# Contracting two key groups of an input projection in halves, the first halves beside the modulation that produces their operand

## The chip, the cores and the metric

One core of a Trainium2 chip runs the whole program once. The metric is the device time of one execution in microseconds (us). The engines are TensorE (PE in the profile, PEld for its weight loads), VectorE (DVE), ScalarE (ACT), GpSimd (POOL) and SyncE (SP), which here only issues DMA transfers. Each engine takes its instructions in the order in which they stand in its queue.

## The reference

A diffusion backbone of two layers works on 256 latent and 256 context tokens of width 2048. The first layer begins so:

```python
sh1, sc1, g1, sh2, sc2, g2 = jnp.split(silu(c) @ ada_w[l] + ada_b[l], 6, axis=-1)
h  = rmsnorm(x_lat, norm_mix[l]) * (1 + sc1) + sh1        # 256 x 2048
hc = the same for x_ctx, with c_ctx                       # 256 x 2048
# even mixer: one input projection, then segments ka, va, kb, vb, a, b, qa, qb, za
pc = hc @ w_in[:, :n_ctx];  p = h @ w_in
ka, va, qa = silu(depthwise_conv(5 taps))                 # gated DeltaNet: k, v, q
k = rope(l2norm(heads(ka)))                               # 8 heads of 128
```

Then come the chunked gated delta rule in both directions (first the context tokens, whose final state starts the latent ones), neighbourhood attention, an output projection, a gated feed-forward part, and the second layer with a short convolution in place of the mixer.

## The kernel before

A product in float32 is made of three TensorE products: weights and activations are split into a high part (`whi`, `h_hi`) and the rest (`wlo`, `h_lo`), and high x high, high x low and low x high are summed in PSUM. ScalarE makes `whi` (L173), VectorE subtracts for the first 576 columns of `wlo` (L241) and GpSimd for the other 448 (L243). Weight tiles of 128 x 1024 (two of the 16 contraction steps of a 512-column group) come through a ring of four `raw` buffers, and two `whi` and two `wlo`.

`fm_stream` (L297 on) contracts one group of 512 columns: a step of it takes one block of 128 rows of `h`, and issues 24 matmuls of 128 x 256 (L311), or 20 with four 512-wide ones (L307) in the first step. It holds four PSUM banks (`mm`, four in all) until `evac` has taken them. The last two steps are issued together, bank by bank.

The program opens with the first modulation, in eight blocks. `start_block(b)` loads 4 MB of `ada_w` (tile `araw0`, four buffers) and multiplies it by the two condition vectors (L484, tile `gd`); `start_tokens(b)` copies the result (L490, `mrow`), turns it to columns (L495), transposes two blocks of normalised tokens (L192, `xn`) and makes blocks 2b and 2b+1 of `h` (L508 to L510, tiles `hlhi`, `hchi`, `hllo`, `hclo`, and `h0` for block 0). So block k of `h` exists only after modulation block k // 2. After each of the first seven blocks, two steps of the first key group (KA0, `s0`, columns C_KA on) are issued on the blocks of `h` just made. After the eighth, `drive(s0)` issues the last two steps, and the second key group (KA1) follows in 16 steps, with one step of a later modulation (`pump`; its DVE part is L338) to each.

`head_evac` (L568) takes a key group further: it copies the four PSUM banks to SBUF (`hst`, alternately on ScalarE and VectorE), and defers nine pieces of work that `drive` spreads over the next steps: for each of the four heads the convolution (`cv`, L560 to L565), then transposes, squares and their sums (L591, L592), and last the norm and the rotation (L606 to L617) and a store to DRAM (`kd`). Behind KA1 stand the gates: a small product (L690 to L698) and a chain of small VectorE operations (L710 to L750), and then what is still deferred. `chunk_matrices(1)` and `inverses` (L862 to L898) use KA0 and KA1 from `kd`; the streams of the query and value groups (QA, VA) are written after them in the program.

The program text gives each instruction a place, and the framework's scheduler, which has a timing model of its own, moves instructions past each other to fill what it takes for gaps. So the order in each queue is that of the built program, not of the text.

Of the kernel before, what the change touches and what calls it, by code (L numbers as in the profile page):

```python
# [29 lines left out]
D = 2048  # L30
KT = D // 128
FH = 5632
# [77 lines left out]
def body(tc, x, c, ctx, c_ctx, ada_w, ada_b, norm_mix, norm_ffn, ffn_w_gate, ffn_w_up, ffn_w_down,  # L110
# [186 lines left out]
    def fm_stream(segs, ks, ws, evac, cut=None):  # L297

        ps = [None] * 4
        for i, group in grouped(((k, (k, hi, lo)) for k, hi, lo in w_steps(segs, ks, cut)), len(ks)):  # L300
            for f in range(4):
                if i == 0:
                    ps[f] = mmt()
                for g, (k, hi, lo) in enumerate(group):
                    a, b = hi[:, f * 128:(f + 1) * 128], lo[:, f * 128:(f + 1) * 128]
                    if i == 0:
                        PE.matmul(ps[f][:, 0:len(ws) * 256], a, h0[:, 0:len(ws) * 256], start=True, stop=False)  # L307
                    for j, (wt, mv) in enumerate(((a, h_hi), (a, h_lo), (b, h_hi))):
                        for n, w in enumerate(ws):
                            if j or i:  # L310
                                PE.matmul(ps[f][:, n * 256:(n + 1) * 256], wt, mv(w, k), start=False,  # L311
                                          stop=i == len(ks) - 1 and g == len(group) - 1 and j == 2 and w == ws[-1])
                if i == len(ks) - 1:
                    evac(f, ps[f])
# [109 lines left out]
    h0 = hlp.tile([128, 512], F32R, name="h0")  # L424
    hs_hi = (hlp.tile([128, KT - 1, 256], F32R, name="hlhi"), hcp.tile([128, KT - 1, 256], F32R, name="hchi"))
    hs_lo = (hlp.tile([128, KT, 256], F32R, name="hllo"), hcp.tile([128, KT, 256], F32R, name="hclo"))

    def h_hi(w, k):
        return hs_hi[w][:, k - 1, :] if k else h0[:, w * 256:(w + 1) * 256]
# [8 lines left out]

    st = Stack()
# [48 lines left out]
    def start_tokens(b, pr):  # L488
        mrow = sp.tile([128, 512], F32, name="mrow", tag="mrow", bufs=2)
# [12 lines left out]
        for k in range(2 * b, 2 * b + 2):  # L502
# [3 lines left out]
            for w in range(2):  # L506
                m = sp.tile([128, 256], F32, name="modt", tag="modt", bufs=4)
# [4 lines left out]
    def token_stats():  # L512
# [5 lines left out]
        junk = sp.tile([128, D], F32, name="junk")  # L518
# [49 lines left out]
    def head_evac(n, q, c0, done, sums):  # L568
# [3 lines left out]
        def f(i_, p):  # L572
            st_[i_] = kvp.tile([128, 512], F32, name="hst", tag="hst", bufs=4)[:, 0:n * 128]
            copy(st_[i_], p[:, 0:n * 128])
# [52 lines left out]
    def ka_evac(q):  # L627
# [3 lines left out]
        return head_evac(4, q, 0, done, True)  # L631
# [20 lines left out]

    sums = start_block(0)
    token_stats()
    s0 = fm_stream([(wv, C_KA, 512)], ks, [0, 1], ka_evac(0))
    for b in range(8):
        start_tokens(b, sums)
        if b < 7:
            next(s0), next(s0)
            sums = start_block(b + 1)  # L660
    st.close()
    rstk = Stack()
# [13 lines left out]
    drive(fm_stream([(wv, C_KA + 512, 512)], ks, [0, 1], ka_evac(1)), pump, R_KA)  # L676
# [175 lines left out]
    def inverses(parts, q):  # L852
# [7 lines left out]
        xdT = gw.tile([128, 16, 128], F32, name="xdT", tag="xdT", bufs=XDT)  # L860
# [539 lines left out]
```

## Time and profile before

| | |
|---|---|
| three runs | 2948.97, 2952.24 and 2953.81 us; median 2952.24 us |
| profiled execution | 2949.88 us, of it a span of 2947.9 us from its first to its last instruction |
| busy share of the span | PE 94%, PEld 78%, DVE 65%, ACT 45%, POOL 20% |
| read from DRAM | 657.63 MB, 230 GB/s over the span |

The span is that of the instructions of the program; the time of the execution is 2.0 us longer. A matmul counts as busy from its issue to its modelled end, and the next is issued before that, so the busy share of PE is not its use: what it lost is read from the idle time before its instructions, and from the granted clock. The changed part of the program lies in the first 150 us; what follows from it reaches to about 480 us.

### The profile page before, as it was taken

How to read it: one execution, taken by the hardware profiler on the slowest of the kernel's cores; microseconds unless marked ns; L12 is line 12 of the kernel's file. 1: busy time of each engine (PE TensorE's matmuls, PEld its weight loads, DVE VectorE, ACT ScalarE, POOL GpSimd, SP SyncE). 2: the span in 40 equal slices, each digit the busy share in tenths (PEclk: the TensorE clock that was granted, in tenths of full speed). 3: DMA queues.
4: the chain of work that ended last, by engine and by line, in shares of the span. 5: the costliest groups of instructions: out<-in, count | busy, mean ns of one | idle time of the engine just before them, and what ended most of it. 6: DMA issues, size and time to landing. Idle time of an engine off the chain costs nothing. (4 is left out here: it accounts for less than half of the span.)

```text
span 2947.9 us, 40712 instructions
## 1 busy us (share of the span) xinstructions
PE 2764.4 (94%) x15113; PEld 2295.6 (78%) x15113; DVE 1901.8 (65%) x2409; ACT 1337.0 (45%) x1822; POOL 596.2 (20%) x431
## 2 busy tenths in 40 slices
PE   6998888989899899999999998899999999999997
PEld 3697888978777778888878777777778888888886
DVE  2378786744457777666777767777767546445675
ACT  3245444333355444544445555344454444444554
POOL 1157535335241111100111101111111001000010
PEclk9998999999999999999999999999999999999999
DMA  9955657765657688877778766878658657656553
GB/s 343 289 162 160 185 177 251 232 205 184 180 155 262 236 298 294 293 266 270 268 273 274 252 204 234 285 268 297 211 177 315 199 184 257 188 182 220 192 192 123
DMA packets 284930, 680.82 MB, mean 231 GB/s; under 512 B 57273, under 2 KB 97313, under 8 KB 283323
## 3 DMA queue, kind: packets, MB, share of 16 engines
q1 hardware_dynamic: 262148, 652.48, 66.6%
q10 hardware_dynamic: 22583, 25.73, 2.9%
q8 instruction: 119, 1.95, 0.3%
q14 instruction: 80, 0.66, 0.1%
HBM read 657.63 MB, written 20.48 MB: 230 GB/s over the span
## 5 line engine op out<-in xcount | busy, mean ns | idle before, releaser
L241 DVE TENSOR_TENSOR wlo<-raw,whi 128x1024 fp32r<-128x1024 f32 (+1 forms) x800 | 998.0, 1260 | 530.7 <-ACT whi L173 499.2
L173 ACT ACTIVATE whi<-raw 128x1024 fp32r<-128x1024 f32 x800 | 835.8, 1056 | 668.0 <-PE mm L285 479.4
L338 DVE SCALAR_TENSOR_TENSOR acc<-araw,cT,acc 128x1024 f32<-128x1024 f32 (+1 forms) x312 | 366.5, 1175 | 248.7 <-DMA araw<-in_ada_w_dram 222.3
L283 PE MATMUL mm<-wlo,fhi 128*128 128x512 f32 x1232 | 477.7, 393 | 2.1 <-DVE wlo L241 2.0
L282 PE MATMUL mm<-whi,fhi 128*128 128x512 f32 x1232 | 475.9, 397 | 0.0
L285 PE MATMUL mm<-whi,flo 128*128 128x512 f32 x1232 | 392.4, 392 | 0.0
L336 POOL TENSOR_TENSOR acc<-araw,acc 128x1024 f32<-128x1024 f32 (+1 forms) x78 | 159.0, 2039 | 1068.6 <-ACT araw L335 599.5
L283 PEld LDWEIGHTS mm<-wlo,fhi 128*128 128x128 f32 x1232 | 232.4, 189 | 53.7 <-DVE wlo L241 5.0
L285 PEld LDWEIGHTS mm<-whi,flo 128*128 128x128 f32 x1232 | 231.6, 188 | 50.6
L282 PEld LDWEIGHTS mm<-whi,fhi 128*128 128x128 f32 x1232 | 232.7, 189 | 48.4
L282 PE MATMUL mm<-whi,ahi 128*128 128x512 f32 x672 | 262.3, 395 | 4.0 <-DVE rtmp L1157 2.9
L283 PE MATMUL mm<-wlo,ahi 128*128 128x512 f32 x672 | 261.9, 393 | 0.2 <-DVE wlo L241 0.2
L243 POOL TENSOR_TENSOR wlo<-raw,whi 128x448 fp32r<-128x448 f32 x112 | 163.4, 1460 | 285.7 <-ACT whi L173 267.3
L285 PE MATMUL mm<-whi,alo 128*128 128x512 f32 x672 | 211.7, 395 | 2.8 <-DVE alo L177 2.6
L335 ACT ACTIVATE araw<-araw,cT 128x1024 f32<-128x1024 f32 (+1 forms) x78 | 74.4, 954 | 256.3 <-DMA araw<-in_ada_w_dram 235.2
L311 PE MATMUL mm<-hllo,whi 128*128 128x256 f32 x640 | 184.1, 293 | 0.0
L311 PE MATMUL mm<-hlhi,wlo 128*128 128x256 f32 x600 | 168.3, 296 | 14.1 <-DVE wlo L241 10.6
L311 PE MATMUL mm<-hlhi,whi 128*128 128x256 f32 x600 | 170.4, 296 | 5.8 <-ACT whi L173 4.2
L1159 POOL TENSOR_TENSOR xs<-rtmp,xs 128x512 f32<-128x512 f32 x24 | 35.4, 1493 | 633.2 <-DVE rtmp L1157 631.9
L282 PEld LDWEIGHTS mm<-whi,ahi 128*128 128x128 f32 x672 | 127.0, 189 | 32.9 <-issue 3.4
L285 PEld LDWEIGHTS mm<-whi,alo 128*128 128x128 f32 x672 | 126.2, 189 | 32.7 <-DVE alo L177 5.7
L283 PEld LDWEIGHTS mm<-wlo,ahi 128*128 128x128 f32 x672 | 126.8, 189 | 29.5 <-DVE wlo L241 2.0
(398 smaller groups left out, 4694.0 us busy)
## 6 DMA issues: line engine op xcount, KB each, us to landing
araw<-in_ada_w_dram SPq DMA_DIRECT2D x288, 512.0 KB
raw<-in_ffn_w_down_dram SPq DMA_DIRECT2D x176, 512.0 KB
raw<-in_ffn_w_gate_dram SPq DMA_DIRECT2D x160, 512.0 KB
raw<-in_ffn_w_up_dram SPq DMA_DIRECT2D x160, 512.0 KB
raw<-in_ev_w_in_dram SPq DMA_DIRECT2D x112, 512.0 KB
araw<-in_ada_w_dram SPq DMA_DIRECT2D x192, 256.0 KB
raw<-in_od_w_in_dram SPq DMA_DIRECT2D x96, 512.0 KB
raw<-in_ev_w_out_dram SPq DMA_DIRECT2D x32, 512.0 KB
```

What stands on the lines that cost most here:

```text
L173: ACT.activation(dst, src, AF.Copy)
L241: DVE.tensor_tensor(lo[:, 0:cut], raw[:, 0:cut], hi[:, 0:cut], op=OP.subtract)
L243: POOL.tensor_tensor(lo[:, cut:], raw[:, cut:], hi[:, cut:], op=OP.subtract)
L282: PE.matmul(ps[ti][n], a, hi[:, n * 512:(n + 1) * 512], start=first, stop=False)
L283: PE.matmul(ps[ti][n], a, lo[:, n * 512:(n + 1) * 512], start=False, stop=False)
L285: PE.matmul(ps[ti][n], b, hi[:, n * 512:(n + 1) * 512], start=False, stop=last)
L311: PE.matmul(ps[f][:, n * 256:(n + 1) * 256], wt, mv(w, k), start=False, stop=i == len(ks) - 1 and g == len(group) - 1 and j == 2 and w == ...
L335: ACT.activation(raw, raw, AF.Copy, scale=col)
L336: POOL.tensor_tensor(acc2, raw, acc2, op=OP.add)
L338: DVE.scalar_tensor_tensor(acc, raw, col, acc, op0=OP.mult, op1=OP.add)
L1159: eng.tensor_tensor(v, tmp, v, op=OP.add)
```

## The change

`fm_stream` is called four times in place of two. `half(c0)` contracts the first eight blocks of `h` for KA0 and then for KA1 and copies the four sums of each to SBUF (`part`, 128 x 4 x 512). `ka_evac` of the second halves adds `part` to the PSUM bank (one VectorE operation a bank, line 584 of the changed kernel) where it copied the bank before. The modulation blocks 0 to 2 issue two steps each as before, and the blocks 3 to 6 four in place of two: 22 in place of 14. Block 8 of `h` gets a 512-wide tile of its own (`h8`), since it opens a stream now. `mrow` has one buffer in place of two, `modt` three in place of four, and the scratch of the token statistics lies in `hllo`. `part` takes the two buffers of `xdT`, which `inverses` uses later.

```diff
-                        PE.matmul(ps[f][:, 0:len(ws) * 256], a, h0[:, 0:len(ws) * 256], start=True, stop=False)
+                        PE.matmul(ps[f][:, 0:len(ws) * 256], a, lead[k][:, 0:len(ws) * 256], start=True, stop=False)
...
-    h0 = hlp.tile([128, 512], F32R, name="h0")
+    lead = {k: hlp.tile([128, 512], F32R, name=f"h{k}") for k in (0, KH)}
...
+    rstk = Stack()
+    xp = pool("sums", stack=rstk, side="right")
...
-        mrow = sp.tile([128, 512], F32, name="mrow", tag="mrow", bufs=2)
+        mrow = sp.tile([128, 512], F32, name="mrow", tag="mrow", bufs=1)
...
-                m = sp.tile([128, 256], F32, name="modt", tag="modt", bufs=4)
+                m = sp.tile([128, 256], F32, name="modt", tag="modt", bufs=3)
...
-        junk = sp.tile([128, D], F32, name="junk")
+        junk = hs_lo[0][:, 0:KH, :].rearrange("p k t -> p (k t)")
...
-            copy(st_[i_], p[:, 0:n * 128])
+            if part is None:
+                copy(st_[i_], p[:, 0:n * 128])
+            else:
+                DVE.tensor_tensor(st_[i_], p, part[:, i_, :], op=OP.add)
...
+    def half(c0):
+
+        part = xp.tile([128, 4, 512], F32, name="part", tag="xdT", bufs=XDT)
+        return part, fm_stream([(wv, c0, 512)], ks[:KH], [0, 1], lambda f, p: copy(part[:, f, :], p))
...
-    s0 = fm_stream([(wv, C_KA, 512)], ks, [0, 1], ka_evac(0))
+    p0, a0 = half(C_KA)
+    p1, a1 = half(C_KA + 512)
+    s0 = fm_stream([(wv, C_KA, 512)], ks[KH:], [0, 1], ka_evac(0, p0))
+    plan = [s for s, n in ((a0, KH), (a1, KH), (s0, KH)) for _ in range(n)]
     for b in range(8):
         start_tokens(b, sums)
         if b < 7:
-            next(s0), next(s0)
+            for _ in range((2, 2, 2, 4, 4, 4, 4)[b]):
+                next(plan.pop(0))
             sums = start_block(b + 1)
...
-    drive(fm_stream([(wv, C_KA + 512, 512)], ks, [0, 1], ka_evac(1)), pump, R_KA)
+    drive(fm_stream([(wv, C_KA + 512, 512)], ks[KH:], [0, 1], ka_evac(1, p1)), pump, R_KA)
...
-        xdT = gw.tile([128, 16, 128], F32, name="xdT", tag="xdT", bufs=XDT)
+        xdT = xp.tile([128, 16, 128], F32, name="xdT", tag="xdT", bufs=XDT)
```

So in the changed program the queues stand otherwise from the fifth modulation block on. TensorE, in the kernel before, around the columns of that block (`mrow`): the matmuls of the modulation (`gd`) stand right before those that turn its result.

```order
L311 MATMUL mm<-hlhi,wlo 128x256
L311 MATMUL mm<-hchi,wlo 128x256
L484 MATMUL gd<-araw_663,cT_120 32x512 x4
L484 MATMUL gd<-araw_670,cT_120 32x512 x4
L484 MATMUL gd<-araw_677,cT_120 32x512 x4
L495 MATMUL sm<-cs,mrow 128x2 x4
L192 MATMUL sm<-cs,xn 128x128 x4
L484 MATMUL gd<-araw_776,cT_120 32x512 x4
```

TensorE of the changed kernel at the same place (the lines have other numbers: 501 is L495 of before, 193 is L192, 312 is L311):

```order
L312 MATMUL mm<-hllo,whi 128x256
L312 MATMUL mm<-hclo,whi 128x256
L312 MATMUL mm<-hlhi,wlo 128x256
L312 MATMUL mm<-hchi,wlo 128x256
L312 MATMUL mm<-hlhi,whi 128x256
L312 MATMUL mm<-hchi,whi 128x256
L501 MATMUL sm<-cs,mrow 128x2 x4
L193 MATMUL sm<-cs,xn 128x128 x4
L312 MATMUL mm<-hllo,whi 128x256
L312 MATMUL mm<-hclo,whi 128x256
```

Here 26 matmuls of a key group stand between the last `gd` and `mrow`, and 18 between the two halves of the transposes; it is so in the fifth, sixth and seventh block. In the eighth `mrow` follows `gd` directly, as before.

VectorE of the changed kernel, where KA1's sums are taken from PSUM (line 584 is the new addition, 569 is L563 of before, a tap of the convolution, 339 is L338, the pump, 242 is L241, a weight split, 602 is L592):

```order
L242 TENSOR_TENSOR wlo<-raw,whi 128x576
L584 TENSOR_TENSOR hst<-mm,part 128x512
L339 SCALAR_TENSOR_TENSOR acc<-araw,cT,acc 128x512
L584 TENSOR_TENSOR hst<-mm,part 128x512
L569 SCALAR_TENSOR_TENSOR cv<-hst,evcT,cv 128x2x255
L602 TENSOR_REDUCE hss<-sq 128x4
L339 SCALAR_TENSOR_TENSOR acc<-araw,cT,acc 128x512
L569 SCALAR_TENSOR_TENSOR cv<-hst,evcT,cv 128x2x254
L242 TENSOR_TENSOR wlo<-raw,whi 128x576
L339 SCALAR_TENSOR_TENSOR acc<-araw,cT,acc 128x512
L569 SCALAR_TENSOR_TENSOR cv<-hst,evcT,cv 128x2x254
L584 TENSOR_TENSOR hst<-mm,part 128x512
```

The convolution of KA0 is still under way there; in the kernel before it was complete when KA1's copies stood in this queue.

TensorE of the kernel before in the first inverse of the context tokens (L883, L890 and L896 are its products), with matmuls of the value stream between them:

```order
L890 MATMUL gd<-xdT,Y 32x32 x32
L896 MATMUL gd<-Y,xdT 32x32 x32
L192 MATMUL sm<-cs,cv 128x128 x4
L883 MATMUL gd<-xd,n_2286 64x64
L311 MATMUL mm<-hlhi,whi 128x256
L311 MATMUL mm<-hllo,whi 128x256
L311 MATMUL mm<-hlhi,whi 128x256
L311 MATMUL mm<-hllo,whi 128x256
```

TensorE of the changed kernel there (902, 909 and 915 are L883, L890 and L896 of before):

```order
L902 MATMUL gd<-xd,n_2274 32x32
L193 MATMUL sm<-cs,cv 128x128 x4
L902 MATMUL gd<-xd,n_2274 32x32 x31
L909 MATMUL gd<-xdT,Y 32x32 x32
L915 MATMUL gd<-Y,xdT 32x32 x32
L902 MATMUL gd<-xd,n_2273 64x64 x16
L909 MATMUL gd<-xdT,Y 64x64 x16
L308 MATMUL mm<-h_100,whi 128x256
```

In the kernel before 64 matmuls of streams stand within the first inverse and 34 within the second; in the changed one none and 81.

## Rows read from the trace of the kernel before

**Rows 1.** The page, part 1: busy us (share), instructions

```profile
PE 2764.4 (94%) x15113; PEld 2295.6 (78%) x15113; DVE 1901.8 (65%) x2409; ACT 1337.0 (45%) x1822; POOL 596.2 (20%) x431
```

**Rows 2.** Stretches: us, busy us (instructions) by engine, PEclk, DMA share, GB/s

```profile
89.00:144.00 55.00, 48.94 (x362) 33.44 (x361) 18.35 (x52) 12.17 (x20) 10.77 (x7) 0.94 0.90 284
...
144.00:222.00 78.00, 74.10 (x600) 72.68 (x600) 60.19 (x88) 34.57 (x47) 41.46 (x32) 0.98 0.52 163
222.00:300.00 78.00, 65.34 (x471) 62.65 (x470) 67.74 (x110) 43.52 (x69) 57.31 (x52) 0.89 0.49 156
300.00:480.00 180.00, 154.95 (x1642) 149.28 (x1642) 137.09 (x233) 80.27 (x124) 83.99 (x79) 0.95 0.64 196
```

**Rows 3.** PE in order of time: start, us, instruction, [idle before <-releaser]

```profile
71.59 0.28 PE L311 MATMUL mm<-hclo,whi 128*128 128x256 f32 x1
71.71 0.28 PE L311 MATMUL mm<-hlhi,wlo 128*128 128x256 f32 x1
...
92.44 1.07 PE L484 MATMUL gd<-araw,cT 128*32 128x512 f32 x8 [1.27 <-DMA araw<-in_ada_w_dram]
94.42 1.84 PE L495 MATMUL sm<-cs,mrow 128*128 128x2 f32 x8 [0.91 <-DVE mrow L490]
...
140.06 0.74 PE L311 MATMUL mm<-hlhi,whi 128*128 128x256 f32 x4 [1.17 <-DVE hlhi L509]
```

**Rows 4.** One stretch more, columns as in rows 2

```profile
94.20:101.00 6.80, 6.58 (x30) 4.62 (x31) 1.99 (x9) 1.80 (x4) 0.00 (x0) 0.50 1.08 355
```

**Rows 5.** Waits of PE from 89 to 144 us: total us, times, longest

```profile
PE sm L495 <- DVE mrow L490: 3.6, 4, 0.9
```

**Rows 6.** Stretches, DVE alone: us, busy us, PEclk, DMA share, GB/s

```profile
144.00:180.00 36.00, 34.46 (x39) 1.00 0.62 193
180.00:222.00 42.00, 25.72 (x50) 0.96 0.44 137
222.00:297.00 75.00, 66.52 (x104) 0.89 0.48 152
```

**Rows 7.** DVE in order of time: KA0's copy, gates, KA1's rotation

```profile
144.98 0.69 DVE L170 COPY hst<-mm 128x512 f32<-128x512 f32 x1 [2.78 <-PE mm L311]
...
210.27 0.29 DVE L710 COPY ab<-sm 128x128 f32<-128x128 f32 x1 [3.51 <-PE sm L698]
...
223.04 0.29 DVE L740 SCALAR_TENSOR_TENSOR g_t<-gu,ea 128x32 f32<-128x32 f32 x2
...
295.62 1.37 DVE L617 TENSOR_TENSOR hq<-hq,rope 128x256 f32<-128x256 f32 x1
```

**Rows 8.** Groups of DVE, 144 to 297 us: count | busy us, mean ns | idle

```profile
L241 DVE TENSOR_TENSOR wlo<-raw,whi 128x576 fp32r<-128x576 f32 x26 | 28.2, 1084 | 12.6 <-ACT whi L173 12.5
L338 DVE SCALAR_TENSOR_TENSOR acc<-araw,cT,acc 128x512 f32<-128x512 f32 x24 | 24.5, 1022 | 0.5 <-DMA araw<-in_ada_w_dram 0.5
...
L170 DVE COPY hst<-mm 128x512 f32<-128x512 f32 x4 | 2.7, 683 | 2.8 <-PE mm L311 2.8
...
L592 DVE TENSOR_REDUCE hss<-sq 128x2 f32<-128x256 f32 x4 | 1.6, 406 | 0.0
```

**Rows 9.** Lines 241 and 338 (140 to 300 us) and 1157: ns min/median/max

```profile
L241 DVE TENSOR_TENSOR wlo<-raw,whi x26: 745/810/1703, 151.4 to 294.9; 128x576 fp32r<-128x576 f32 x26
...
L338 DVE SCALAR_TENSOR_TENSOR acc<-araw,cT,acc x24: 653/764/1645, 146.7 to 289.6; 128x512 f32<-128x512 f32 x24
...
L1157 DVE TENSOR_TENSOR rtmp<-mm,row x32: 673/681/692, 939.9 to 2932.8; 128x512 f32<-128x512 f32 x32
```

**Rows 10.** POOL in order of time: the clearing of xdT

```profile
136.31 3.54 POOL L862 MEMSET xdT<- 128x2048 f32 x2
```

**Rows 11.** PE in the two inverses, 429 to 459 us, as rows 3

```profile
429.11 0.72 PE L890 MATMUL gd<-xdT,Y 32*32 32x32 f32 x62 [1.64 <-ACT Y L173]
...
435.07 0.30 PE L883 MATMUL gd<-xd,n 64*64 64x64 f32 x2 [3.69 <-DVE xd L898]
...
458.58 0.37 PE L896 MATMUL gd<-Y,xdT 32*32 32x32 f32 x19 [3.26 <-issue]
```

More of the change, by code (lines that the diff above doesn't have):

```diff
@@ L31 @@
 KT = D // 128
+KH = KT // 2
 FH = 5632
@@ L422, in body @@
     hcp = pool("h_ctx", stack=hcstk)
-    h0 = hlp.tile([128, 512], F32R, name="h0")
-    hs_hi = (hlp.tile([128, KT - 1, 256], F32R, name="hlhi"), hcp.tile([128, KT - 1, 256], F32R, name="hchi"))
+    lead = {k: hlp.tile([128, 512], F32R, name=f"h{k}") for k in (0, KH)}
+    hs_hi = (hlp.tile([128, KT - 2, 256], F32R, name="hlhi"), hcp.tile([128, KT - 2, 256], F32R, name="hchi"))
     hs_lo = (hlp.tile([128, KT, 256], F32R, name="hllo"), hcp.tile([128, KT, 256], F32R, name="hclo"))
     def h_hi(w, k):
-        return hs_hi[w][:, k - 1, :] if k else h0[:, w * 256:(w + 1) * 256]
+        if k in lead:
+            return lead[k][:, w * 256:(w + 1) * 256]
+        return hs_hi[w][:, k - 1 - (k > KH), :]
     def h_lo(w, k):
@@ L566, in conv_silu, with head_evac @@
         return o
-    def head_evac(n, q, c0, done, sums):
+    def head_evac(n, q, c0, done, sums, part=None):
         st_ = {}
@@ L625, in to_features, with ka_evac @@
             copy(dst[:, g * 2:g * 2 + 2, :], pt.rearrange("p (i e) -> p i e", i=2))
-    def ka_evac(q):
+    def ka_evac(q, part=None):
         def done(kt, ss):
@@ L630, in done @@
             ACT.dma_start(hslice(kd, 0, 4, q), kt.rearrange("p t h e -> p t (h e)"))
-        return head_evac(4, q, 0, done, True)
+        return head_evac(4, q, 0, done, True, part)
     def va_evac(q):
@@ L658, in body @@
         if b < 7:
-            next(s0), next(s0)
+            for _ in range((2, 2, 2, 4, 4, 4, 4)[b]):
+                next(plan.pop(0))
             sums = start_block(b + 1)
     st.close()
-    rstk = Stack()
     adap = pool("ada", stack=rstk, side="right")
```

## The prediction

> **What bounds the kernel now.** I read the page first: TensorE is busy 94% of the span [rows 1], so over the whole program the question is where TensorE still loses time. I then cut the stretch that the change can reach into four windows [rows 2]. From 89 to 144 us the second half of the modulation runs; DMA is at 0.90 of its engines there and moves 284 GB/s, and it moves 355 GB/s where it is full [rows 4]. So TensorE and DMA are both near their limits, and neither leaves much room. From 222 to 300 us TensorE is held by others: VectorE is busy 67.7 of 78 us and the granted clock is 0.89 [rows 2].
>
> TensorE's own rows come next [rows 3]. Two matmuls of 128 x 256 start 0.12 us apart, so a step of 24 takes 2.9 us. Before the columns of every modulation block it waits 0.91 us for VectorE's copy; from 89 to 144 us this happens four times, 3.6 us in all [rows 5]. Once it waits 1.27 us for `ada_w` and right after it 0.91 us for the copy, and from 94.2 us on the granted clock is at its lower level, 1.2 GHz, for 6.8 us [rows 3, 4]. After the last block it waits 1.17 us for `h` [rows 3]. Last I read VectorE by stretch [rows 6]: from 144 to 180 us it is full (34.5 of 36 us, the convolutions of KA0), from 180 to 222 us it is idle for 16.3 us, since KA1's sums are not there yet, and from 222 to 297 us it is idle for 8.5 us.
>
> **What moves.** Before the eighth block's `h`, TensorE issues 14 steps now (20 + 13 x 24 = 332 matmuls) and 22 after the change (188 + 188 + 140 = 516). The 184 more cost 184 x 0.12 = 22.1 us [rows 3]. All matmuls stay: what the modulation gains, the rest of KA1 loses. So the gain isn't 22.1 us but only what idle time they cover.
>
> **What they cover.** In the changed order 26 matmuls (3.1 us) stand before the columns in three of the four last blocks, so three waits of 0.91 us go: 2.7 us. The `gd` products of the fifth block stand behind 44 matmuls of KA1, 5 us later, so the wait of 1.3 us for `ada_w` goes too. The lower clock came right behind these two waits; 6.8 us at half speed lose 3.4 us, and I count them as saved. Together 7.4 us. If the clock falls all the same, it is 4.0 us. The last block's waits stay (0.9 and 1.2 us).
>
> DMA must bring four more weight tiles there, 4 x 0.5 = 2.1 MB. At 284 GB/s over 55 us it has (355 - 284) x 55 = 3.9 MB of room [rows 2, 4], and the stretch gets longer as well, so I cost this at nothing. On SP the tiles stand between the loads of the modulation; a weight load waits there for the ring of four `raw`, and each is freed by a step that TensorE has behind it before the next `gd`, so nothing is held up behind it. If this cover were gone, 2.1 MB at 355 GB/s is 5.9 us.
>
> **What comes later.** KA0's last step ends 22.1 - 7.4 = 14.7 us later: VectorE takes its first bank at 145.0 + 14.7 = 159.7 us [rows 7]. From there KA0's convolutions, the gates and KA1's convolutions follow, and KA1's half has eight steps fewer under which to do it. I follow VectorE from this bank to the last rotation of KA1, behind which `kd` is stored. Now this takes from 145.0 to 297.0 us, 152.0 us [rows 7], of which it is idle 1.5 + 16.3 + 8.5 = 26.3 us [rows 6], so 125.7 us are work.
>
> Its work in the changed order up to the same place: 21 weight splits in place of 26, -5 x 1.08 us; 19 pump steps in place of 24, -5 x 1.02; no copies in place of four, -2.7; eight additions [rows 8]. An addition from PSUM with another operand in SBUF stands at L1157, 0.68 us [rows 9]: +5.4. Of the query group one sum (0.4) and five small operations, of under 0.2 us each by my estimate from it, come forward: +1.3. The sum is -5.4 - 5.1 - 2.7 + 5.4 + 1.3 = -6.5 us. Bounds of the additions: the copy's 0.68 from below, and from above a weight split's mean of 1.08 (+3.2 us in all); I take L1157, which has the same operands.
>
> On those durations there is a rule to weigh. Splits last 0.75 to 1.70 us and pump steps 0.65 to 1.65, while L1157 keeps within 0.67 to 0.69 [rows 9]. The Trainium skill, page "GPSIMD Engine Reference", section "1. Specifications", says that GpSimd shares its SBUF interfaces with VectorE and contends with VectorE instructions that have two inputs in SBUF. By that rule the splits and pump steps are long because GpSimd works beside them, and the additions stay short; the trace agrees. Without such a stretching the sum would be -3.7 - 3.3 - 2.7 + 5.4 + 1.3 = -3.0 us and the result of this part -1.6 in place of -5.1.
>
> Idle time is the open term. The 16.3 us from 180 to 222 us were a wait for KA1's matmuls, and these are now half as many (22.1 us less), so I keep 3 us of them: 1.5 + 3 + 8.5 = 13 us. Then the last rotation ends at 159.7 + 125.7 - 6.5 + 13 = 291.9 us, 5.1 us earlier than now. If all 26.3 us stay, it ends 8.2 us later; if only the last 8.5 stay, 9.6 us earlier.
>
> **Small edits.** GpSimd cleared both `xdT` at 136 us, 3.5 us, when it had nothing else [rows 10]. Now each clearing waits until VectorE has added the sums, and a weight split and a square stand behind it: at most 1.8 us each, which I count within the 3 us above. One `mrow` is enough, since the matmuls that read it are over a block earlier; with three `modt`, ScalarE's fourth waits for VectorE's first subtraction, and VectorE is the slower there, so nothing moves. The scratch in `hllo` is read before the first block writes there: nothing. The five pump steps are done later, beside streams in which VectorE is busy 137 of 180 us [rows 2]: nothing.
>
> **At the inverses.** In the first one 64 stream matmuls, 7.7 us, stood between its dependent products, and TensorE still waited 1.6 + 3.7 us [rows 11]; now none stand there, so up to 7.7 us more are open. In the second there are 47 more (5.6 us), over a wait of 3.3 us. Between -3.3 and +4.4 us; I take +1.5.
>
> **The sum.** -5.1 + 1.5 = -3.6 us. Against the profiled execution (2949.88 us) this is 2946.3 us. That execution was 2.4 us below the median of the runs, 2952.24, so the time to expect beside it is 2948.6 us. A measurement can tell about 0.2%, 5.9 us, from no change.
>
> **Rivals.** *The idle time of VectorE goes.* KA1's half is short enough, VectorE works through, and only 8.5 us are left: -9.6 us, with the inverses at -1: 2941.6 us. For it: 16.3 us idle now, with one clear cause. Against: the order on each queue is fixed, and a wait for ScalarE or GpSimd remains. Chance 0.22.
>
> *The wait only changes its name.* Half of KA1's matmuls are earlier, but the convolutions of KA0 begin 14.7 us later and TensorE waits at their transposes, where it lost little before; VectorE's idle time stays at 18 us: 296.9 us, as now, and 2952 to 2953 us. For it: from 144 to 180 us VectorE was already full. Chance 0.20.
>
> *VectorE holds TensorE's banks: slower.* KA1's banks are all taken by VectorE now, and its additions stand in the queue behind convolutions and pump steps of KA0; the query stream needs these banks, and TensorE has no other work in front. Then its small product for the gates comes late, VectorE waits for that in turn, and the 26.3 us of idle time stay: +8.2 + 1.5 = +9.7, 2962 us; at the worse end of the inverses 2965. It decides from 19 us of idle time on, where the sum reaches zero. For it: four banks, all in one queue that was full from 144 to 180 us [rows 6]. Against: four copies on ScalarE go, and five pump steps are put off. Chance 0.15.
>
> **How the numbers follow.** My forecast, 2948.6 us, has chance 0.43, and its own range is 2944 to 2953. With the first rival at 0.22 and the last at 0.15, a range of 2939 to 2960 leaves out about a tenth on either side. Faster by over 0.2% (under 2946.3): nearly all of the first rival and a third of the forecast, 0.37. Slower by over 0.2% (over 2958.1): the last rival and a little of the second, 0.17. Within: 0.46.
>
> **What would show it.** In the changed profile: no wait before the columns in the blocks four to six and the full clock around 94 us (else the 7.4 us are wrong); KA0's first addition at about 160 us; VectorE's idle time from there to KA1's last rotation (13 us, and that at about 292 us); TensorE's waits for the transposes of the convolutions and for `hst` around 185 to 200 us, which should stay below some 5 us; a longer wait in the first inverse and a shorter in the second. If the total moves by more than 10 us either way, the idle time of VectorE was misjudged.

## The result and the profile after

The changed kernel takes 2961.45 us (median of 8 runs, 2953.04 to 2968.18); the kernel before, run beside it, takes 2952.49 us (8 runs, 2941.87 to 2956.78). The ratio is 1.0037, with a 95% interval of 1.0024 to 1.0050: slower by 7 to 15 us. The forecast was 2948.6 us, and the range ended at 2960.

The profiled execution of the changed kernel took 2953.04 us, the shortest of its eight; that of the kernel before, 2949.88, lay 2.6 us below its median. So the two traces differ by only 3.2 us of the 9, and what is read from them is checked below on other kernels. First the page, part 1, and four stretches of the span (columns as in [rows 2]), which answer to [rows 1, 2]:

```profile
PE 2755.8 (93%) x15105; PEld 2292.2 (78%) x15105; DVE 1898.0 (64%) x2417; ACT 1338.5 (45%) x1823; POOL 590.2 (20%) x431
```

```profile
89.00:144.00 55.00, 55.00 (x441) 44.01 (x440) 19.32 (x46) 14.40 (x22) 11.46 (x7) 1.00 0.88 280
144.00:222.00 78.00, 65.94 (x500) 61.04 (x498) 58.36 (x89) 31.93 (x44) 35.57 (x28) 0.93 0.47 141
222.00:300.00 78.00, 62.89 (x485) 60.87 (x486) 64.09 (x120) 44.09 (x69) 54.21 (x55) 0.96 0.49 154
300.00:480.00 180.00, 147.22 (x1506) 140.73 (x1505) 138.03 (x223) 75.11 (x119) 85.20 (x77) 0.93 0.65 194
```

From 89 to 144 us TensorE (first column) has no gap and the full clock. From 144 to 222 us it is busy 65.9 us where it was 74.1, and from 300 to 480 us 147.2 where it was 155.0; with 100 and 136 matmuls fewer in these stretches, that alone is no loss. What is lost is counted below.

The waits of TensorE in the modulation, 89 to 158 us (total us, times, longest), answer to [rows 3, 5]:

```profile
PE sm L501 <- DVE mrow L496: 0.9, 1, 0.9
PE mm L312 <- DVE hlhi L515: 0.5, 1, 0.5
```

Three of the four waits for `mrow` are gone, that for `ada_w` too. VectorE in order of time, KA0's four additions and KA1's last rotation, answers to [rows 7], and its stretches to [rows 6]:

```profile
159.99 2.48 DVE L584 TENSOR_TENSOR hst<-mm,part 128x512 f32<-128x512 f32 x4 [2.97 <-PE mm L312]
...
297.33 0.42 DVE L627 TENSOR_TENSOR hq<-hq,rope 128x256 f32<-128x256 f32 x1
```

```profile
160.00:297.70 137.70, 115.94 (x192) 0.94 0.46 142
160.00:180.00 20.00, 18.60 (x23) 1.00 0.57 167
180.00:222.00 42.00, 35.44 (x53) 0.88 0.37 115
222.00:297.70 75.70, 61.91 (x117) 0.95 0.48 151
```

KA0's sums come at 160.0 us, as forecast; the last rotation ends at 297.7 us, 0.7 us later than before and not 5.1 earlier. What came between stands on TensorE, at the end of KA1 and the start of the query group:

```profile
184.66 0.28 PE L312 MATMUL mm<-hchi,wlo 128*128 128x256 f32 x1
188.93 0.55 PE L308 MATMUL mm<-h,whi 128*128 128x256 f32 x1 [4.00 <-ACT whi L174]
189.28 0.41 PE L312 MATMUL mm<-hllo,whi 128*128 128x256 f32 x1
189.50 0.41 PE L312 MATMUL mm<-h,wlo 128*128 128x256 f32 x1
...
198.65 0.28 PE L312 MATMUL mm<-hllo,whi 128*128 128x256 f32 x1
198.76 0.28 PE L312 MATMUL mm<-hlhi,wlo 128*128 128x256 f32 x1
200.67 0.66 PE L193 MATMUL sm<-cs,cv 128*128 128x128 f32 x4 [1.62 <-ACT cv L571]
```

and on VectorE, which takes KA1's banks behind a pump step that waits for its operand:

```profile
182.53 1.63 DVE L339 SCALAR_TENSOR_TENSOR acc<-araw,cT,acc 128x512 f32<-128x512 f32 x1 [3.83 <-DMA araw<-in_ada_w_dram]
...
188.11 0.68 DVE L584 TENSOR_TENSOR hst<-mm,part 128x512 f32<-128x512 f32 x1
...
189.79 0.68 DVE L584 TENSOR_TENSOR hst<-mm,part 128x512 f32<-128x512 f32 x1
...
195.24 0.68 DVE L584 TENSOR_TENSOR hst<-mm,part 128x512 f32<-128x512 f32 x1
...
199.92 0.69 DVE L584 TENSOR_TENSOR hst<-mm,part 128x512 f32<-128x512 f32 x1
```

KA1's last matmul is issued at 184.66 us. Its first bank is free at 188.8 (188.11 + 0.68), and TensorE goes on at 188.93. The row names ScalarE's `whi`, since a weight split of ScalarE ends at 188.8 too (187.75 + 1.04), so this trace alone can't tell which of the two held TensorE. In five other kernels with the move and the additions (e1, e9, e13, e15, e16) the same wait, of 2.9 to 3.9 us, is put down to the bank; here e13:

```profile
188.32 0.55 PE L308 MATMUL mm<-h,whi 128*128 128x256 f32 x1 [3.66 <-DVE hst L584]
```

Behind the 4.0 us the matmuls stand 0.21 us apart in place of 0.12 until 198.3: the lower clock.

Further on TensorE waits for convolved heads, whose transposes (`cv`, `hq`) it has to do. From 140 to 300 us, the kernel before and then the changed one:

```profile
PE mm L311 <- DVE wlo L241: 3.6, 3, 2.2
PE sm L192 <- ACT cv L565: 3.4, 5, 1.1
```

```profile
PE sm L193 <- ACT cv L571: 10.1, 5, 3.3
PE mm L312 <- DVE wlo L242: 5.8, 4, 2.4
PE mm L308 <- ACT whi L174: 4.0, 1, 4.0
PE mm L312 <- POOL wlo L244: 2.8, 1, 2.8
```

and from 300 to 480 us, in the same order:

```profile
...
PE sm L192 <- DVE hq L617: 4.1, 2, 3.5
...
PE sm L192 <- ACT cv L565: 2.9, 3, 1.4
```

```profile
PE sm L193 <- DVE hq L627: 7.7, 4, 3.2
PE sm L193 <- ACT cv L571: 6.6, 4, 3.0
```

With the smaller rows of the same kind (0.9 us for `hq` in the first stretch of the changed kernel) the waits for heads are 3.4 + 4.1 + 2.9 = 10.4 us before and 10.1 + 0.9 + 7.7 + 6.6 = 25.3 us after.

The first product of the first inverse, before and after:

```profile
421.89 0.22 PE L883 MATMUL gd<-xd,n 32*32 32x32 f32 x2 [0.54 <-DMA xd<-dz]
```

```profile
445.96 0.24 PE L902 MATMUL gd<-xd,n 32*32 32x32 f32 x2 [0.38 <-DMA xd<-dz]
```

Ahead of it VectorE solves small triangular systems by substitution (`sub_tmp`, `zsol`), from 346.0 to 406.8 us before and from 351.6 to 429.8 us after. The costliest other groups of VectorE in these two stretches:

```profile
L563 DVE SCALAR_TENSOR_TENSOR cv<-hst,evcT,cv 128x508 f32<-128x508 f32 (+1 forms) x17 | 14.0, 844 | 0.0
L338 DVE SCALAR_TENSOR_TENSOR acc<-araw,cT,acc 128x512 f32<-128x512 f32 x7 | 7.5, 1071 | 0.0
L241 DVE TENSOR_TENSOR wlo<-raw,whi 128x576 fp32r<-128x576 f32 x8 | 6.9, 864 | 0.0
```

```profile
L569 DVE SCALAR_TENSOR_TENSOR cv<-hst,evcT,cv 128x508 f32<-128x508 f32 (+1 forms) x25 | 21.9, 890 | 0.4 <-ACT cv L566 0.4
...
L242 DVE TENSOR_TENSOR wlo<-raw,whi 128x576 fp32r<-128x576 f32 x12 | 14.0, 1165 | 0.4 <-ACT whi L174 0.4
...
L339 DVE SCALAR_TENSOR_TENSOR acc<-araw,cT,acc 128x512 f32<-128x512 f32 x13 | 11.6, 893 | 0.4 <-DMA acc<-in_ada_b_dram 0.4
```

Taps, weight splits and pump steps of the later groups stand between the steps of the substitution: 32 before, 50 after.

### The profile page after: what moved, and what is told of

Same layout as the page of the kernel before. It is cut to its first block, busy times and chain, and to the rows that moved or that the text cites. A ratio compares the mean times of both kernels' runs of the same rounds, so it can differ in the third digit from the quotient of the medians.

```text
span 2951.2 us, 40709 instructions
## 1 busy us (share of the span) xinstructions
PE 2755.8 (93%) x15105; PEld 2292.2 (78%) x15105; DVE 1898.0 (64%) x2417; ACT 1338.5 (45%) x1823; POOL 590.2 (20%) x431
## 5 line engine op out<-in xcount | busy, mean ns | idle before, releaser
L339 DVE SCALAR_TENSOR_TENSOR acc<-araw,cT,acc 128x1024 f32<-128x1024 f32 (+1 forms) x312 | 358.9, 1150 | 275.6 <-DMA araw<-in_ada_w_dram 245.6
L312 PE MATMUL mm<-hlhi,whi 128*128 128x256 f32 x560 | 160.5, 296 | 1.0 <-DVE hlhi L515 1.0
L312 PE MATMUL mm<-hlhi,wlo 128*128 128x256 f32 x560 | 154.1, 294 | 7.2 <-DVE wlo L242 4.2
```

The lines of the kernel that those rows point to most:

```text
L339: DVE.scalar_tensor_tensor(acc, raw, col, acc, op0=OP.mult, op1=OP.add)
```

## The experiments

Theory A is VectorE's chain, which starts late; B the pump steps put off; C the small edits; D the halves themselves; N the order that the scheduler makes. A2 and A3 are what the runs left of A.

A measure is needed that doesn't depend on where work was moved. For each kind of matmul (its shape and its tiles) I took the interval to the next one that a fifth of its kind, in the traces of the kernel before and the changed one together, keep below; what an interval is longer than that is lost, by a wait or by the lower clock. Added up this is TensorE's lost time; by 160 us every kernel has ended the modulation. All kernels:

| kernel | ratio to before (95%) | lost to 160 us | 160 to 220 | 220 to 480 | first inverse at | third at |
|---|---|---|---|---|---|---|
| before | 1 | 72.5 | 6.7 | 72.3 | 421.9 | 621.8 |
| changed | 1.0037 (1.0024 to 1.0050) | 63.8 | 16.1 | 80.9 | 446.0 | 635.2 |
| e2 small edits alone | 1.0000 (0.9986 to 1.0014) | 71.9 | 6.9 | 73.1 | 420.0 | 620.0 |
| e3 halves, no move | 1.0044 (1.0029 to 1.0059) | 70.0 | 7.0 | 82.2 | 439.5 | 643.0 |
| e10 additions alone | 1.0044 (1.0028 to 1.0059) | 70.6 | 7.5 | 80.5 | 441.3 | 645.1 |
| e18 VectorE copies alone | 1.0047 (1.0028 to 1.0065) | 73.6 | 10.5 | 79.1 | 447.9 | 651.1 |
| e11 changed, no additions | 1.0070 (1.0055 to 1.0085) | 64.0 | 16.7 | 84.7 | 443.8 | 644.7 |
| e4 a quarter of KA1 | 1.0084 (1.0068 to 1.0101) | 65.7 | 10.3 | 80.5 | 442.6 | 647.0 |
| e1 changed, pump 16 | 1.0039 (1.0025 to 1.0054) | 65.0 | 16.0 | 81.8 | 437.6 | 630.3 |
| e7 before, VectorE loaded | 1.0124 (1.0107 to 1.0141) | 73.4 | 10.9 | 82.0 | 459.5 | 668.7 |
| e6 before, half the taps | 1.0070 (1.0050 to 1.0091) | 75.4 | 6.0 | 75.9 | 429.6 | 634.2 |
| e5 changed, half the taps | 0.9974 (0.9961 to 0.9986) | 66.1 | 11.0 | 63.8 | 415.0 | 605.9 |
| e8 before, pump late | 1.0021 (1.0007 to 1.0035) | 72.2 | 6.8 | 64.0 | 409.1 | 619.6 |
| e9 changed, pump late | 1.0102 (1.0087 to 1.0117) | 66.1 | 15.7 | 81.8 | 430.8 | 649.2 |
| e12 before, VA 0.7 | 1.0001 (0.9989 to 1.0013) | 71.5 | 8.3 | 70.1 | 421.9 | 618.6 |
| e13 changed, VA 0.7 | 1.0035 (1.0021 to 1.0048) | 64.5 | 15.9 | 75.5 | 442.9 | 632.8 |
| e14 before, QA 0.6 | 1.0067 (1.0048 to 1.0086) | 74.7 | 5.8 | 76.1 | 434.4 | 644.8 |
| e15 changed, QA 0.6 | 1.0090 (1.0074 to 1.0106) | 64.4 | 15.8 | 85.6 | 443.0 | 639.0 |
| e17 before, pump on GpSimd | 1.0021 (1.0008 to 1.0035) | 75.9 | 8.8 | 77.7 | 429.9 | 630.9 |
| e16 changed, pump on GpSimd | 1.0086 (1.0065 to 1.0107) | 64.2 | 14.9 | 88.0 | 443.3 | 648.0 |

Times are us; 0.0010 is 3 us. The third inverse is the first of the latent tokens. Each profile is one execution, so a difference of 2 or 3 us in one cell says nothing. The profiles of e6 and e5 lie 15 and 10 us below the median of their runs, that of e18 10 us above. Nor do the three columns add up to the time: by the same measure the difference to the kernel before behind 480 us is -4 us in the changed kernel, +17 in e4 and e8 and +23 in e9.

### Parts of the change alone

**e2_side.** The kernel before with the small edits: `mrow` 1, `modt` 3, the scratch in `hllo`, `xdT` from its own pool.

> The kernel before with the small edits alone: mrow one buffer, modt three, the scratch of the statistics in hllo, xdT from a pool of its own. Theory C (the small edits cost): slower by some 5 to 9 us. Theories A and B: within 3 us of the kernel before, KA0's first copy at 145 +-1 us, the last rotation of KA1 at 297 +-2 us.

Measured: ratio 1.0000. The small edits cost nothing. KA0's first copy and the last rotation came about 2 and 3 us earlier than expected (142.6 and 293.9 us).

**e3_nomove.** The halves without the move; KA1's first half runs behind the modulation.

```diff
-    plan = [s for s, n in ((a0, KH), (a1, KH), (s0, KH)) for _ in range(n)]
+    plan = [s for s, n in ((a0, KH), (s0, KH)) for _ in range(n)]
...
-            for _ in range((2, 2, 2, 4, 4, 4, 4)[b]):
+            for _ in range((2, 2, 2, 2, 2, 2, 2)[b]):
...
+    drive(a1, pump, R_KA)
```

> The changed kernel with the halves but without the move: the modulation issues 14 steps as before, all of KA0 (its two halves), and both halves of KA1 follow behind it with a pump step each. Theory A: KA0's first addition is back at 145 to 147 us, and the time is that of the kernel before plus the price of the halves on VectorE (eight additions in place of four copies, and half of eight part copies: 5.4 - 2.7 + 2.7 = 5.4 us of work, of which idle time takes some), so +0 to +4 us: 2952 to 2956 us. Theory D (the halves themselves, the additions and the part sums, cost the 9 us): 2958 to 2963 us. Theory C: as the changed kernel.

Measured: 2965.02 us, 2 us above theory D's range, and as slow as the changed kernel or slower. Up to 220 us it loses what the kernel before does (77.0 and 79.2 us); from 220 to 480 us it loses 10 us more. So the move isn't needed for the loss, and the direct price of the halves (5.4 us) is less than it.

**e10_add_only.** No halves: whole streams, and their banks are taken with an addition of zeros. The cut below is against the kernel before, without e2's small edits and the addition in `head_evac`.

```diff
+    def zero():
+        part = xp.tile([128, 4, 512], F32, name="part", tag="xdT", bufs=XDT)
+        POOL.memset(part, 0.0)
+        return part
...
-    s0 = fm_stream([(wv, C_KA, 512)], ks, [0, 1], ka_evac(0))
+    s0 = fm_stream([(wv, C_KA, 512)], ks, [0, 1], ka_evac(0, zero()))
...
-    drive(fm_stream([(wv, C_KA + 512, 512)], ks, [0, 1], ka_evac(1)), pump, R_KA)
+    drive(fm_stream([(wv, C_KA + 512, 512)], ks, [0, 1], ka_evac(1, zero())), pump, R_KA)
```

> The kernel before with the small edits and with additions: KA0 and KA1 are contracted in one piece as before, but the four sums of each are taken from PSUM by VectorE with the addition of a tile of zeros, which takes the two buffers of xdT until then. So eight additions stand in place of four VectorE and four ScalarE copies; nothing else. Theory D1 (VectorE taking all eight banks, and GpSimd's clearing of xdT behind it, is what the halves cost): 2957 to 2964 us, the first inverse 10 us or more later than 421.9 us. Theory D2 (it is the shorter streams, which change where the pieces of work put off fall): 2948 to 2954 us.

Measured: 2963.20 us, in theory D1's range; e3's ratio, and its columns. VectorE's stretch from KA0's first bank to the end of the substitution before the inverses is 271.2 us in e10, 269.7 in e3 and in the changed kernel, 261.6 before. On SyncE seven other loads stand between the result of the substitution (`dz`) and the loads that the first inverse waits for, where one stood. The kernel before, and then e10:

```profile
406.82 0.71 SPq L849 DMA_DIRECT2D dz<-zsol  x1
408.52 0.59 SPq L849 DMA_DIRECT2D dz<-lsol  x1
410.75 1.68 SPq L330 DMA_DIRECT2D araw<-in_ada_w_dram  x1
417.72 1.21 SPq L867 DMA_DIRECT2D xdT<-dz  x2
```

```profile
414.52 0.70 SPq L858 DMA_DIRECT2D dz<-zsol  x1
415.70 0.53 SPq L230 DMA_DIRECT2D raw<-in_ev_w_in_dram  x1
416.34 2.58 SPq L330 DMA_DIRECT2D araw<-in_ada_w_dram  x1
419.01 2.42 SPq L858 DMA_DIRECT2D dz<-lsol  x1
...
428.70 0.38 SPq L788 DMA_DIRECT2D vtok<-vd__142  x1
429.19 0.42 SPq L230 DMA_DIRECT2D raw<-in_ev_w_in_dram  x1
432.40 0.87 SPq L876 DMA_DIRECT2D xdT<-dz  x2
```

From `dz` to the first product of the inverse it is 27 us there (414.5 to 441.3), 15 before (406.8 to 421.9). In the changed kernel it is 16 us (429.9 to 446.0), with five other loads: what delays the inverse in e10 is not what delays it there.

**e18_dve_copies.** Less still: e2, and VectorE copies all eight banks.

```diff
-            copy(st_[i_], p[:, 0:n * 128])
+            (DVE.tensor_copy if c0 == 0 else copy)(st_[i_], p[:, 0:n * 128])
```

> The kernel before with the small edits, and VectorE copies all eight banks of KA0 and KA1 (four of them were ScalarE's): no additions, no second operand, xdT cleared early as before. Theory V (VectorE taking all banks is what costs in e10_add_only): 2959 to 2966 us, the first inverse some 20 us later than 421.9 us, and as many other loads on SyncE between the stores of the substitution and the inverse's loads. Theory X (the late clearing of xdT and the shared buffers): 2946 to 2954 us, the first inverse within 4 us of 421.9 us.

Measured: 2963.18 us, theory V. Four copies of 0.68 us, 2.7 us in all, go from ScalarE to VectorE, and the whole is 14 us slower (ratio 1.0047). VectorE's stretch is 273.9 us, from `dz` to the inverse it is again 27 us (420.6 to 447.9). So three kernels that share, beside the small edits, only this, that VectorE takes all the banks of KA0 and KA1, have the same loss and the same order on SyncE. But seven other loads stand there in e14 too, which takes the banks as before (`dz` at 413.1, the inverse at 434.4): the order is the scheduler's answer to an edit, and more than one edit brings it.

**e11_halves_noadd.** The changed kernel, with the banks copied by ScalarE and VectorE in turn (the first halves' sums are left out of the result).

```diff
-                DVE.tensor_tensor(st_[i_], p, part[:, i_, :], op=OP.add)
+                copy(st_[i_], p)
```

> The changed kernel without the additions: the second halves' sums are copied from PSUM by ScalarE and VectorE in turn as in the kernel before, and the first halves' sums are left out of the result. Theory D1: ScalarE takes half of the banks, KA1's banks come free up to 5 us earlier, VectorE has four instructions less, and the loss is at least halved: 2950 to 2956 us. Theory D2: as the changed kernel, 2957 to 2964 us.

Measured: 2971.70 us, worse than the changed kernel. Neither theory said that. What costs 13 us when it is added to the kernel before gives nothing back when it is taken from the changed one: the losses don't add up. TensorE waits 1.3 us for banks behind KA1 there, and 2.2 us for a weight split of VectorE.

**e4_quarter.** Four steps of KA1 ahead of an undivided KA0, 18 steps in the modulation.

```diff
-KH = KT // 2
+KH = KT // 4
...
-    s0 = fm_stream([(wv, C_KA, 512)], ks[KH:], [0, 1], ka_evac(0, p0))
-    plan = [s for s, n in ((a0, KH), (a1, KH), (s0, KH)) for _ in range(n)]
+    s0 = fm_stream([(wv, C_KA, 512)], ks, [0, 1], ka_evac(0))
+    plan = [s for s, n in ((a1, KH), (s0, KT)) for _ in range(n)]
...
-            for _ in range((2, 2, 2, 4, 4, 4, 4)[b]):
+            for _ in range((2, 2, 2, 3, 3, 3, 3)[b]):
```

> Only the first four steps of KA1 are put beside the modulation, ahead of KA0, and one step more stands in the blocks 3 to 6 (2,2,2,3,3,3,3: 18 steps); KA0 is contracted in one piece, without part sums. Theory A: four steps more cost 4 x 2.9 = 11.8 us of TensorE and save the waits before the columns and at the clock (up to 7.4 us), so KA0's first copy comes at 149 to 152 us, 4 to 7 us later than before in place of 15; four additions only. The loss should be less than half: 2950 to 2957 us. If the loss came from KA1's halves or from the reordered inverses, it stays about 9 us: 2958 to 2963 us.

Measured: 2974.82 us, out of both ranges. KA0's first copy came at 150.1 us, as expected, and up to 160 us four steps save 6.8 us of the 8.7 that eight save. From 160 to 220 us it loses 3.6 us more than the kernel before, from 220 to 480 us 8.2, and from 700 to 1000 us another 8.5 (58.7 for 50.2). A smaller move doesn't lose less.

### VectorE's load

**e7_delay.** The kernel before, with KA0's first convolution done six times (`for _ in range(6 if ft == 0 else 1)` around the four taps and the ScalarE operation that opens them).

> The kernel before, and the convolution of KA0's first head is done six times, so 20 taps of 0.74 us, some 15 us, more for VectorE right behind KA0's sums; nothing is halved or moved, TensorE's work is the same. Theory A: the end of the substitution, 406.6 us in the kernel before, comes 10 to 16 us later, the first inverse too, and the whole is 7 to 14 us slower: 2957 to 2964 us. Theory N: VectorE's 43 us of idle time take it up, 0 to 4 us slower.

Measured: 2984.23 us, far above both ranges. The load of some 15 us cost 35 us: VectorE's stretch is 290.4 us, and the first inverse is 38 us later. VectorE's idle time took up nothing: 42 us of it stayed, of 43. The edit isn't taps alone: each round opens with a ScalarE operation that waits for the taps before it, and ScalarE's weight splits stand behind it.

**e6_taps_before, e5_taps_after.** Two of four taps left out for all heads, in both kernels.

```diff
-        for i in (0, 1, 3, 4):
+        for i in (1, 3):
```

> The kernel before with two of VectorE's four convolution taps left out for every head, so part of the computation is missing. Theory A (VectorE's queue from KA0's first bank to the end of the substitution before the inverses, 262 us in the kernel before, 270 in the changed one, and 43 us of it idle in both, holds up the inverses and with them the end): some 40 taps of 0.75 to 0.98 us go from this stretch; it gets 15 to 35 us shorter, the first inverse starts as much earlier than 421.9 us, and the whole is 8 to 25 us faster than the kernel before, 2927 to 2943 us. Theory N (VectorE's queue is not what holds the end; the loss is in how the streams happen to lie among the dependent products): within 4 us of the kernel before.

> The changed kernel with the same two taps left out for every head. Theory A: the changed kernel's loss came from VectorE's later start; with 30 us less work on VectorE its idle time can take up part of the 15 us, so it stands nearer to e6_taps_before than the changed kernel stands to the kernel before: 0 to 6 us slower than that one (against 9 to 11), and 10 to 30 us faster than the changed kernel. Theory N: no tie to VectorE, 5 to 15 us slower than e6_taps_before, and within 4 us of the changed kernel.

Measured: 2970.63 and 2942.86 us. The kernel before gets slower with less work; its VectorE stretch stays 262.6 us, of which 66 are idle (43 in the kernel before). The changed kernel gets faster than anything else here, with 235.8 us for the stretch. TensorE's waits for heads up to 480 us fall there to 14.1 us from 25.3. So less work on VectorE helps the changed kernel and hurts the other: its amount alone doesn't decide.

**e8_pumplate, e9_after_pumplate.** Fewer pump steps early, more late (`R_KA = 0.5`, `R_QA = 0.25`, `R_KB` 1.55 and 1.6).

> The kernel before with fewer pump steps beside KA1 (0.5 to a step in place of 1) and the query groups (0.25 in place of 0.5), made up beside the later key and value groups (1.55 in place of 1.3): 16 pump steps of 1.0 us go from ahead of the substitution's end, where VectorE now does 36. Theory A: that end comes 8 to 16 us earlier than 406.6 us and the whole is 3 to 10 us faster, 2941 to 2948 us, unless the later groups lose it. Theory N: within 3 us of the kernel before.

> The changed kernel with fewer pump steps beside KA1 (0.5 to a step in place of 1) and the query groups (0.25 in place of 0.5), made up later (1.6 in place of 1.3): some 12 pump steps of 1.0 us go from VectorE's queue ahead of the substitution's end, 429.7 us in the changed kernel. Theory A2 (KA0's sums come 15 us later, the stretch from them to the inverses doesn't get shorter, and an inverse that starts later than in the kernel before, 421.9 us, costs; one that starts earlier gains nothing): the first inverse starts 8 to 20 us earlier than 446 us and most of the loss goes, 2948 to 2956 us. Theory N (the loss lies in how the streams happen to stand in the queues, not in when the inverses start): 2957 us or more.

Measured: 2954.93 and 2981.61 us. Both first inverses start 13 to 15 us earlier than in the kernels without the edit, as expected, and both are slower than those. An earlier first inverse alone is worth nothing; theory A2 falls. In e8 the 8 us that TensorE gains up to 480 us are lost again behind it.

**e16_after_pool, e17_before_pool.** A third of VectorE's pump steps go to ScalarE and GpSimd.

```diff
-                elif k % 4 == 1:
+                elif k % (2 if width < 1024 else 4) == 1:
```

> The changed kernel, and of 16 pump steps of a 512-wide block 8 in place of 12 are VectorE's; the other 4 go the way of every fourth step now, ScalarE (0.72 us) and GpSimd (1.6 us). About 12 us less for VectorE up to the substitution's end, 19 us more for GpSimd. Theory A3 (the move fails because TensorE is early and waits for VectorE at the convolved heads and the weight splits, 25.3 us at the heads up to 480 us against 10.4 before): the wait at the heads falls to 14 to 20 us, and the whole is 5 to 15 us faster than the changed kernel, 2946 to 2956 us. If GpSimd becomes the hold-up (it is busy 54 of 78 us from 222 to 300 us), it is slower than the changed kernel.

> The kernel before with the same share of pump steps. Theory A3: little to gain, since TensorE waits for the heads only 10.4 us there: 2944 to 2954 us, so the distance of the pair falls below the 7 to 11 us that the other pairs show. Theory N: any value from -3 to +25 us, and the distance of the pair has no tie to VectorE's work.

Measured: 2975.98 and 2958.98 us. Both are slower, and the waits for heads hardly fall (23.5 us in e16): theory A3 falls as a rule on VectorE's work.

### Pump rates

**e1_pump16.** `R_KA = 2.0` in the changed kernel, as many pump steps beside KA1 as before.

> The changed kernel with two pump steps to each of the eight remaining steps of KA1 (R_KA 2.0), so that as many stand there as in the kernel before. Theory A (VectorE's chain: KA0's sums come 15 us later, VectorE is the bound from there to KA1's last rotation, and what TensorE gained goes into waits for KA1's banks and for the convolutions): five to eight pump steps of 1.0 us more stand in VectorE's queue in that stretch, the last rotation comes 3 to 8 us later than 297.7 us, and the whole is slower than the changed kernel by 0 to 8 us, so 2961 to 2969 us against 2952 before. Theory B (the pump steps put off are what costs, since they meet the inverses and the scans): the loss goes, 2950 to 2954 us.

Measured: 2961.64 us. The last rotation came at 307.5 us, 10 us later, and the time is the changed kernel's. The pump steps put off aren't the cause (theory B falls).

**e12_before_va07, e13_after_va07, e14_before_qa06, e15_after_qa06.** `R_VA = 0.7` or `R_QA = 0.6` in both kernels.

> The kernel before with 0.7 pump steps to a step of the value groups in place of 0.8: three pump steps of 1.0 us are put off, nothing else. Theory A2 (work and waits that can be named make the time): within 4 us of the kernel before, 2946 to 2954 us. Theory N (the order that the scheduler makes behind KA1 makes it, and the kernel before has a good one): any value from -3 to +25 us.

> The changed kernel with the same edit, 0.7 in place of 0.8. Theory A2: 5 to 15 us slower than e12_before_va07, and within 4 us of the changed kernel. Theory N: its distance to e12_before_va07 has no tie to the 9 to 11 us of the pair without the edit.

> The kernel before with 0.6 pump steps to a step of the query groups in place of 0.5: three pump steps of 1.0 us come forward. Theory A2: within 4 us of the kernel before. Theory N: any value from -3 to +25 us.

> The changed kernel with 0.6 in place of 0.5 to a step of the query groups. Theory A2: 5 to 15 us slower than e14_before_qa06, and within 4 us of the changed kernel. Theory N: its distance to e14_before_qa06 has no tie to the 9 to 11 us of the pair without the edit, and the sign may change.

Measured: 2950.26, 2961.09, 2969.04 and 2976.40 us. The pairs lie 0.34 and 0.23% apart, as the pair without an edit does (0.37%); in pairs with larger edits the distance is 0.81 (e9, e8), 0.65 (e16, e17) and -0.96% (e5, e6). Three pump steps brought forward cost the kernel before 0.67%, theory N's range. The pair e12, e13 came as theory A2 said; e14 is 18 us slower than the kernel before and e15 15 us slower than the changed one, where A2 allowed 4.

## Why the prediction was wrong

Two steps failed. The idle time of VectorE up to KA1's last rotation was put at 13 us and was 21.8, which took away the 5.1 us that the forecast lived on. And the end of the program was made to follow that rotation, with the inverses as a term of their own: the rotation moved by 0.7 us, but the first inverse by 24.1.

**Right: the modulation.** The waits and the clock were to give 7.4 us. KA0's sums came 15.0 us later (145.0 to 160.0) for 22.1 us of matmuls: 7.1 us. Every kernel with the whole move loses 63.8 to 66.1 us up to 160 us, those without it 70.0 to 75.9. The single `mrow` and the three `modt` cost nothing (e2), and the four weight tiles that DMA brings more held up nothing there: TensorE has no gap from 89 to 144 us.

**Right: the additions.** Eight took 683 ns each, 5.2 us busy; the sum said 5.4. They lasted 0.68 to 0.69 us, the four beside which GpSimd worked like the other four; of the pump steps from 140 to 300 us in the same trace, those beside GpSimd had a median of 1.36 us and the others 0.74. So the prediction was right to take L1157's duration. VectorE's work from KA0's sums to the last rotation was 115.9 us; the sum said 119.2.

**Right within its bounds: the inverses.** Inside the first two, from their first to their last product, TensorE loses 26.0 us before and 24.6 after; the term was +1.5, between -3.3 and +4.4.

**Wrong: the idle time.** Of VectorE's 26.3 us I let 13 stay, 1.5 + 3 + 8.5; 21.8 stayed, 1.4 (to 180 us) + 6.6 (to 222) + 13.8 (to 297.7). "I keep 3 of them" was 3.6 us short; 5.3 us more came in the last stretch, which I had left as it was. The 16.3 us before weren't one wait either: 8.2 of them were for ScalarE's `whi`, which itself waited mostly for matmuls, and 3.5 for the gates' product. These went, and others took their place: 3.8 us for `araw` right ahead of KA1's additions, and from 222 us on 6.7 us for ScalarE's `em` (the chunk matrices), where it was 1.2. With 8.8 us more idle time and 3.3 us less work the rotation ends 5.5 us later than forecast, and 0.3 us came from KA0's sums: 5.8. (The prediction's own sum reaches zero at 13 + 3.6 = 16.6 us of idle time, not at 19.)

**The third rival had the place, not the size.** TensorE stood still at KA1's first bank, as the rival said, and then ran at the lower clock for 9 us, which it did not foresee. From 160 to 220 us all seven kernels with the whole move and all taps lose 14.9 to 16.7 us; those without it 5.8 to 8.8, and 10.5 and 10.9 in e18 and e7. So the 7 us gained are gone by 220 us: lost time up to there is 79.9 us after and 79.2 before. This is shown by undoing the move: e3 loses 7.0 and keeps the full clock from 160 to 220 us. The additions, the rival's reason, aren't needed for it: e11, without them, loses 16.7, with waits for VectorE's weight split and a granted clock of 0.72 from 185 to 190 us and 0.80 from 190 to 200. But what hangs on the small product for the gates was only 1.7 us late (`ab` at 211.9 us, 210.27 in [rows 7]), and VectorE's idle time fell to 21.8 us, not stayed at 26.3. That the rival's 2962 us met the time is partly chance.

**What no term held: behind the last rotation.** The forecast ended there, but for the inverses themselves. The last rotation moved 0.7 us and the first step of the substitution 5.6 us, but its end 23.0 and the first inverse 24.1 us. So most of the delay, 17.4 us, arises in the substitution: its steps take 78.2 us where they took 60.8, nearly without idle time of VectorE in both, since more work of the later groups stands between them. From 220 to 480 us TensorE loses 8.6 us more. Its waits for convolved heads rise there from 8.4 to 23.7 us, while others fall.

VectorE taking all banks of KA0 and KA1 was enough for a loss of this size: e18, e10 and e3 have one without the move, 6.8 to 9.9 us from 220 to 480 us and 13 to 14 us in the time by their ratios, with waits for heads of 16.5 to 17.1 us from 220 to 480 us. The prediction counted this edit as eight times 0.68 us less four copies. But it isn't shown that the changed kernel loses by the same way: in these three the substitution takes 62.5 to 62.6 us, and the inverse is late behind it, 27 us after `dz`; in the changed kernel that part is 16 us.

**What stays open.** Why 2.7 us on VectorE become 13, and why the changed kernel's substitution is spread out: e1, as slow as the changed kernel, has one of 60.8 us and an inverse at 437.6. The instructions behind KA1 are placed by the scheduler, and all these kernels are placed anew: e18, e10 and e3 share seven other loads on SyncE between `dz` and the inverse's loads, where the kernel before has one. Over the 20 kernels the time goes with the start of the third inverse (correlation 0.89), hardly with that of KA0's sums (0.22). That is a tie, not a cause; the order itself could not be held fixed while an edit was made, so what the edit costs and what its order costs could not be parted. That the changed kernel without additions is slower still (e11) speaks for the order having a large share. No version beat the kernel before with the full computation.

## What to carry to other kernels

Work moved into a gap on one engine gained 7 us here, and the program nothing, since the engine behind it was not waiting for that work alone: follow the second engine's queue to the next product that all wait for, not to the end of the stretch that changed. When a scheduler lays out the program, any edit lays out all that follows; run a neutral edit and the parts alone before a few per mille are put down to the edit, since an edit of three pump steps cost 18 us here and another of the same size nothing. When an operation can run on one engine only, like an addition that replaces copies on two, count it as a move of the copies too.

## What the runs showed of the hardware

After the wait of 4.0 us at 184.9 us TensorE ran 9 us at the lower clock, as it did for 6.8 us from 94.2 us on before; in the profile the stretch from 188.9 to 198.3 us is one row, with a granted clock of 0.50:

```profile
188.90:198.30 9.40, 8.34 (x36) 7.81 (x37) 9.37 (x12) 2.56 (x4) 4.66 (x4) 0.50 0.71 222
```

At half the speed the 8.3 us in which TensorE was busy there cost it 4.2 us by my estimate, as much again as the wait itself. The single runs of the kernel before spread over 11 to 22 us within one series, more than most of the effects studied, so one time or one profile can't tell them.
